# The opening of a decoder-block kernel: who casts the second weight tile, and in which order the first rows are turned

## The chip, the cores and the metric

The kernel runs on one core of one Trainium2 chip. The metric is device time in microseconds (us) of one execution; the time of a kernel is the median of several runs. Engines are named as the profile names them: PE is TensorE (matmuls; PEld its weight loads), DVE is VectorE, ACT is ScalarE, POOL is GpSimd, SP issues most of the DMAs.

## The reference, cut to what matters

One decoder block for 512 rows of 1024 numbers (float32): a convolution mixer and a linear recurrence side by side, merged by gates, then a SwiGLU layer. Only its beginning matters here:

```python
def rmsnorm(x, g):
    xf = x.astype(jnp.float32)
    y = xf * lax.rsqrt(jnp.mean(xf * xf, axis=-1, keepdims=True) + EPS)
    return (y * g.astype(jnp.float32)).astype(x.dtype)
...
    h = rmsnorm(x, norm1_g[l])
    z = h @ w_in[l] + b_in[l]
    z_glu, z_rx, z_rg, z_ga, z_gb = jnp.split(z, split_idx, axis=-1)
    u = z_glu[..., :D_CONV] * jax.nn.sigmoid(z_glu[..., D_CONV:])
    ...
```

## The kernel before, in words

Rows of `x` lie on partitions, four row tiles of 128 rows, each in two halves of 512 columns (`xt[t][h]`). The products need the normalised rows turned, so that the 1024 features lie on partitions: eight feature tiles `c` of 128, each a pair `h1p[c]` of a high part (float32 rounded to the PE's fp32r) and a low part (what the rounding left). Weights are split in the same way: a weight tile of 1024 x 128 is loaded into a `raw` buffer, cast to its high part, and the low part is the difference. A product of one feature tile is three matmuls: weight high by input high, weight high by input low, weight low by input high (24 matmuls for a weight tile).

The kernel's beginning is written out by hand inside `tc.manual_schedule(...)` (L640): in it the order of PE, ACT, DVE and SP is that of the Python code. POOL is left to the planner. After it, the planner orders the rest. The steps are:

1. `WARM = 21` matmuls of ones on ones (L505, 42 passes in the profile), which compute nothing that is used and stand ahead of all else on PE.
2. `norm1_rows(0)`, `norm1_rows(1)` (L591): ACT squares and sums each half (L550, L556), takes the root (L557), DVE inverts it (L558) and scales both halves of the row tile (L595, twice).
3. `rows_turned` (L513): the gain `norm1_g` is turned on PE (L517) and copied by DVE into `par` (L518).
4. `emit_to(1, vec.tensor_copy)`: the first weight tile's high part, cast by DVE (L123); its low part by POOL (L119).
5. `turn_half(..., 0, ...)` (L567) for row tiles 0 and 1: for each `c`, two transposes (L574), one for each row tile, then ACT writes the high part with the gain (L582) and DVE the low part (L583). Four PSUM banks take turns.
6. `emit_to(2, vec.tensor_copy, later)`: the second weight tile's high part, again cast by DVE; its low part is DVE's too, put between the two squares of row tile 2 (L652).
7. The loads of row tiles 2 and 3 and of the parameter rows (SP), `norm1_rows(2)`, `norm1_rows(3)`.
8. `early_mm(0, 0)`: 24 matmuls of the first weight tile on the first 256 rows, with the weight-low ones last; `early_mm(1, 0)`: the same for the second weight tile.
9. `turn_half(..., 1, ...)` for row tiles 2 and 3 (three PSUM buffers in turn), then `early_mm(0, 1)`, the recurrence's small factors, `early_mm(1, 1)`, and the rest of the parameters (L517).

Then the third weight tile follows, with all 512 rows in one matmul.

Of the kernel before, what the change touches and what calls it, by code (L numbers as in the profile page):

```python
# [26 lines left out]
ND = D // P  # L27
# [6 lines left out]
RAW = 4  # L34
HL = 5
AHEAD = 4
WARM = 21

FEW, MANY = 32, 112

# [46 lines left out]
def tile_block(ctx, tc, a, out):  # L87
# [19 lines left out]
    def bank(name):  # L107
        return psum.tile([P, T], F32, tag="mm", name=name)
# [4 lines left out]
    vec, act, pe, pool_e = nc.vector, nc.scalar, nc.tensor, nc.gpsimd  # L113
# [388 lines left out]


    wp = bank2("warm")
    for _ in range(WARM):  # L505
        pe.matmul(wp[:, :P], ones, ones, start=True, stop=True)  # L506

    first = [i for i, (lo, _, _) in enumerate(parts) if lo < n_first]
    load_x(0)
# [11 lines left out]
    def pc(name, i):  # L521
        return par[:, col[name] + i : col[name] + i + 1]


    def mm3(ps, ws, xs, lo_last=False):


        n = 3 * len(ws)
        i = 0
        three = [((wh, xh), (wh, xl), (wl, xh)) for (wh, wl), (xh, xl) in zip(ws, xs)]  # L530
        if lo_last:
            three = [q[:2] for q in three] + [q[2:] for q in three]
        for l, r in (q for qs in three for q in qs):
            pe.matmul(ps, l, r, start=i == 0, stop=i == n - 1)  # L534
            i += 1

    def w_tiles(key, kt, ahead=AHEAD):
        h, l = weights(key, ahead)
        return [(h[:, k, :], l[:, k, :]) for k in range(kt)]
# [21 lines left out]
    def rstd_of(halves, junk, between=None):  # L561
        begun = rstd_begin(halves[0], junk[0])
        if between:
            between()
        return rstd_end(begun, halves[1], junk[1])

    def turn_half(name, rows, gname, dest, hf, bk, some=range(ND), full=None):  # L567

        cs = slice(hf * 256, hf * 256 + 256)
        for c in some:  # L570
            ps = bk[c % len(bk)](f"{name}{hf}{c}")
            for t in range(2):
                src = rows[2 * hf + t][c // 4][:, (c % 4) * P : (c % 4 + 1) * P]
                pe.transpose(ps[:, t * P : (t + 1) * P], src, ident)  # L574
# [7 lines left out]
            act.activation(h, ps[:, :256], AF.Copy, scale=g)  # L582
            last = vec.scalar_tensor_tensor(out=l, in0=ps[:, :256], scalar=g, in1=h.bitcast(F32), op0=ALU.mult, op1=ALU.subtract)  # L583
# [7 lines left out]
    def norm1_rows(t, between=None):  # L591
        junk = [shortt(f"n1j{t}{h}") for h in range(2)]
        r = rstd_of(xt[t], junk, between)
        for h in range(2):
            vec.tensor_scalar(out=xt[t][h], in0=xt[t][h], scalar1=r, scalar2=None, op0=ALU.mult)  # L595

    HALVES = [slice(0, 256), slice(256, 512)]
    EARLY = 1
    EARLY_IN = [(GLU + j + 8 * o) for j in range(EARLY) for o in range(2)]
    early = []  # L600

    def early_mm(i, hf):
        m = EARLY_IN[i]
        if hf == 0:
            early.append((m, w_tiles(f"in{m}", ND, 0), bank(f"z{m}")))
        _, ws, ps = early[i]
        mm3(ps[:, HALVES[hf]], ws, parts_of(h1p, HALVES[hf]), lo_last=hf == 0)


    c4, c8 = (consts.tile([P, NR], F32, name=n) for n in ("c4", "c8"))  # L610
# [3 lines left out]
    def lru_factors(scratch):  # L614

        lam = par[:, col["lru_lambda"] : col["lru_lambda"] + NR]
        e, q, po, cc = (scratch[:, i * NR : (i + 1) * NR] for i in range(4))
        ab, s, s2 = (lru_t[:, i, :] for i in range(3))
        vec.tensor_scalar(out=e, in0=lam, scalar1=-1.0, scalar2=None, op0=ALU.mult)
        vec.tensor_tensor(out=ab, in0=lam, in1=e, op=ALU.max)  # L620
        act.activation(ab, ab, AF.Exp, scale=-1.0)
        for g, name in enumerate(("lru_ba", "lru_bx")):
            vec.tensor_scalar(out=bh[:, g, :], in0=par[:, col[name] : col[name] + NR], scalar1=0.5, scalar2=None, op0=ALU.mult)
        vec.tensor_scalar(out=q, in0=ab, scalar1=2.0, scalar2=None, op0=ALU.add)
        vec.reciprocal(q, q)
# [12 lines left out]

    ET = mybir.EngineType
    with tc.manual_schedule(engines={ET.PE, ET.Activation, ET.DVE, ET.SP}):  # L640
        norm1_rows(0)
        norm1_rows(1)
        rows_turned(0, ROWS[0][1])
        emit_to(1, vec.tensor_copy)
        turn_half("tx", xt, "norm1_g", h1p, 0, [bank, bank, bank, bank2])
        later = Later()
        emit_to(2, vec.tensor_copy, later)
        load_x(2)
        load_x(3)
        for i in first[1:]:  # L650
            load_rows(i)
        norm1_rows(2, lambda: vec.tensor_tensor(**later.operands))  # L652
        norm1_rows(3)
        for i in range(len(parts)):
            if i not in first:
                load_rows(i)
        early_mm(0, 0)
        early_mm(1, 0)
        turn_half("tx", xt, "norm1_g", h1p, 1, [bank2, bank, bank])
        emit_to(3)  # L660
        early_mm(0, 1)
        lru_factors(rows_turned(ROWS[0][1], n_first)[:, 2 * P :])
        emit_to(4)
        early_mm(1, 1)
        rows_turned(n_first, n_rows)
    h1 = parts_of(h1p)

# [623 lines left out]
```

## Time and profile before

| | |
|---|---|
| median of 3 runs | 797.87 us (797.6 to 798.1) |
| the profiled execution | 797.7 us |
| its span, first to last instruction | 795.9 us |
| PE busy | 789.2 us, 99% |
| DVE, ACT, POOL busy | 673.2, 471.7, 228.8 us |

The span is shorter than the time by what lies before the first and after the last instruction. PE's busy time counts a matmul until its modelled end, so that two in a row overlap; where PE starts its next matmul is the better clock. A row of the timeline gives the start in us from the span's start, the time until the group's last end, the engine and line, what is written from what, and in brackets how long the engine sat idle before it and what ended that.

### The profile page before, as it was taken

The numbers are of one execution on the slowest core, as the hardware profiler recorded it, in microseconds if no ns is written. First come the engines' busy times: TensorE is split into PE (matmuls) and PEld (weight loads), VectorE is DVE, ScalarE is ACT, GpSimd is POOL, SyncE is SP. The second block draws the span as 40 slices with busy tenths as digits, with TensorE's granted clock in tenths as the row PEclk, the third lists the DMA queues.
The fourth block names the chain that finished last, engine by engine and source line by source line (L and its number), as shares of the span: only waits on it lengthen the run. The fifth ranks groups of instructions, "written<-read, shape, count | busy, mean of one in ns | idle before, by whom it ended". The sixth has DMA issues, their size and how long they took to land.

```text
span 795.9 us, 12177 instructions
## 1 busy us (share of the span) xinstructions
PE 789.2 (99%) x4369; PEld 690.5 (87%) x4369; DVE 673.2 (85%) x1020; ACT 471.7 (59%) x683; POOL 228.8 (29%) x181
## 2 busy tenths in 40 slices
PE   9999999999999999999999999999999999999997
PEld 8888888888888888888888898999999999888885
DVE  6699899999989988786787889978878887889757
ACT  6646585987768855563335575545455555577443
POOL 1855766797666856030000000000000000000000
PEclk9999999999999999999999999999999999999999
DMA  6945646487555664368847545566555553676652
GB/s 213 257 130 143 187 144 208 121 247 208 173 168 173 213 182 120 128 203 263 276 160 243 172 134 158 131 171 181 155 133 133 133 133 106 210 258 207 198 173 106
DMA packets 184604, 140.29 MB, mean 176 GB/s; under 512 B 14259, under 2 KB 162143, under 8 KB 184543
## 3 DMA queue, kind: packets, MB, share of 16 engines
q1 hardware_dynamic: 183103, 134.27, 55.2%
q0 software_dynamic: 1440, 5.24, 3.5%
q8 instruction: 34, 0.56, 0.3%
q14 instruction: 27, 0.22, 0.1%
HBM read 113.79 MB, written 18.64 MB: 166 GB/s over the span
## 4 chain that ended last, share of the span: by engine, by line
PE 99%; DVE 0%; issue 0%; ACT 0%
PE z L534 36%; PE or L953 13%; PE ft L1080 7%; PE yb L534 7%; PE fa L1080 7%; PE fr L1080 6%; PE ya L534 5%; PE mxr L953 5%; PE fe L1080 4%; PE g L827 3%; PE fb L1080 2%; PE f L534 2%; PE warm L506 1%; PE f L1106 1%; PE tx L574 1%; PE th L574 0%
## 5 line engine op out<-in xcount | busy, mean ns | idle before, releaser
L702 DVE SCALAR_TENSOR_TENSOR cv<-u,par,cv 128x511 f32<-128x511 f32 (+19 forms) x240 | 162.4, 730 | 5.0 <-ACT cv L699 4.7
L119 POOL TENSOR_TENSOR hl_in<-raw_in,hl_in 128x1024 fp32r<-128x1024 f32 x51 | 123.5, 2426 | 83.1 <-ACT hl_in L123 69.6
L355 POOL DMA_DIRECT2D raw_fb<-raw_fb x10 | 8.7, 874 | 298.4 <-DVE raw_fb L357 186.1
L119 POOL TENSOR_TENSOR ows<-ows 128x256 f32<-128x256 f32 x66 | 56.7, 861 | 37.7 <-DMA ows<-in_ffn_w_dram 34.7
L123 ACT CAST hl_ft<-raw_fb 128x1024 fp32r<-128x1024 f32 x40 | 41.8, 1048 | 32.5 <-DVE raw_fb L357 17.0
L123 ACT CAST hl_in<-raw_in 128x1024 fp32r<-128x1024 f32 x50 | 52.1, 1043 | 10.4 <-PE z L534 6.6
L119 DVE TENSOR_TENSOR hl_ft<-raw_fb,hl_ft 128x1024 fp32r<-128x1024 f32 x40 | 48.5, 1220 | 7.0 <-ACT hl_ft L123 6.9
L119 DVE TENSOR_TENSOR hl_fb<-raw_fb,hl_fb 128x1024 fp32r<-128x1024 f32 x30 | 36.6, 1221 | 9.5 <-ACT hl_fb L123 9.3
L357 DVE TENSOR_TENSOR raw_fb<-raw_fb,raw_fb 128x1024 f32<-128x1024 f32 x20 | 24.5, 1225 | 20.3 <-DMA raw_fb<-in_ffn_w_dram 20.0
L534 PE MATMUL z<-h10h,hl_in 128*128 128x512 f32 (+1 forms) x108 | 41.5, 385 | 0.0
L534 PE MATMUL z<-h17h,hl_in 128*128 128x512 f32 (+1 forms) x108 | 41.1, 381 | 0.0
L534 PE MATMUL z<-h13h,hl_in 128*128 128x512 f32 (+1 forms) x108 | 41.1, 381 | 0.0
L534 PE MATMUL z<-h15h,hl_in 128*128 128x512 f32 (+1 forms) x108 | 41.1, 381 | 0.0
L534 PE MATMUL z<-h14h,hl_in 128*128 128x512 f32 (+1 forms) x108 | 41.1, 381 | 0.0
L534 PE MATMUL z<-h16h,hl_in 128*128 128x512 f32 (+1 forms) x108 | 41.1, 381 | 0.0
L534 PE MATMUL z<-h12h,hl_in 128*128 128x512 f32 (+1 forms) x108 | 41.1, 381 | 0.0
L534 PE MATMUL z<-h11h,hl_in 128*128 128x512 f32 (+1 forms) x108 | 41.1, 381 | 0.0
L123 ACT CAST hl_fb<-raw_fb 128x1024 fp32r<-128x1024 f32 x30 | 31.4, 1047 | 8.9 <-PE mxr L953 3.7
L119 DVE TENSOR_TENSOR hl_ob<-raw_ob,hl_ob 128x1024 fp32r<-128x1024 f32 (+1 forms) x23 | 27.0, 1174 | 11.0 <-ACT hl_ob L123 10.9
L123 ACT CAST hl_ob<-raw_ob 128x1024 fp32r<-128x1024 f32 (+1 forms) x23 | 23.3, 1015 | 21.6 <-PE or L953 10.8
L1080 PE MATMUL fe<-hs_0h,hl_ft 128*128 128x256 f32 x160 | 30.7, 283 | 0.0
L1080 PE MATMUL ft<-hs_1h,hl_ft 128*128 128x256 f32 x160 | 30.4, 283 | 0.0
(1016 smaller groups left out, 2610.0 us busy)
## 6 DMA issues: line engine op xcount, KB each, us to landing
raw_in<-in_w_in_dram SPq DMA_DIRECT2D x52, 512.0 KB
raw_fb<-in_ffn_w_dram SPq DMA_DIRECT2D x96, 256.0 KB
ows<-in_ffn_w_dram SPq DMA_DIRECT2D x44, 256.0 KB
os<-ows SPq DMA_DIRECT2D x22, 512.0 KB
raw_ob<-in_ffn_w_dram SPq DMA_DIRECT2D x33, 256.0 KB
raw_ot<-os SPq DMA_DIRECT2D x33, 256.0 KB
raw_lo<-in_lru_w_out_dram SPq DMA_DIRECT2D x16, 320.0 KB
raw_fb<-raw_fb POOLq DMA_DIRECT2D x10, 512.0 KB, 4.6
```

What stands on the lines that cost most here:

```text
L119: return eng.tensor_tensor(out=o, in0=x, in1=y, op=ALU.subtract)
L123: copy(h, full)
L355: pool_e.dma_start(out=q, in_=y, accum_op=ALU.add)
L357: vec.tensor_tensor(out=q, in0=q, in1=y, op=ALU.add)
L506: pe.matmul(wp[:, :P], ones, ones, start=True, stop=True)
L534: pe.matmul(ps, l, r, start=i == 0, stop=i == n - 1)
L574: pe.transpose(ps[:, t * P : (t + 1) * P], src, ident)
L702: vec.scalar_tensor_tensor(out=acc[c][:, s:], in0=u[c][:, : T - s], scalar=dw(c, s), in1=acc[c][:, s:], op0=ALU.mult, op1=ALU.add)
L827: pe.matmul(ps, l, r, start=k == 0, stop=k == len(mms) - 1)
L953: pe.matmul(banks[i], l_[:, ts], r_, start=start and n == 0, stop=stop and n == 2, skip_group_check=again)
L1080: pe.matmul(ps[:, HALVES[i]], lw[:, 4 * i + c, :], rx_, start=not (again or i or c or m), stop=bool(i and c == 3 and m == 2), skip_group_c ...
L1106: pe.matmul(plain_1[:, cs], l, r, start=k == 0 and m == 0, stop=k == ND - 1 and m == 2)
```

## The change

The warming matmuls are cut from 21 to 12 plus 3. After the first 12, the eight transposes of row tile 0 are issued as soon as its rows are scaled; then come the 3 other warming matmuls, the gain's transpose, and the eight transposes of row tile 1. Four PSUM banks hold all of it: bank `c % 4` has feature tile `c` and `c + 4`, each with both row tiles. Only then do ACT and DVE split them (`split_rows`), in the order of `c`.

The high part of the second weight tile is cast by POOL instead of DVE. POOL joins the engines whose order is written out: first this cast, then the low part of the first weight tile. DVE keeps the second tile's low part.

Matmuls of both weight tiles on the first 256 rows are mixed: four feature tiles of the first, then for each further feature tile of the first two of the second; the weight-low matmuls come after these, the second tile's first.

Row tiles 2 and 3 go through ACT and DVE in a slightly different order (`norm1_pair`: the sum of squares of row tile 3 is begun ahead of the scaling of row tile 2). Their transposes are also done row tile by row tile, all sixteen ahead of ACT's and DVE's split.

```diff
-WARM = 21
+WARM = 12, 3
...
-    for _ in range(WARM):
-        pe.matmul(wp[:, :P], ones, ones, start=True, stop=True)
+    def warm_up(n):
+        for _ in range(n):
+            pe.matmul(wp[:, :P], ones, ones, start=True, stop=True)
...
+    def norm1_pair(t, t2, later):
+        jk, jk2 = row_junk(t), row_junk(t2)
+        begun = rstd_begin(xt[t][0], jk[0])
+        vec.tensor_tensor(**later.operands)
+        r = rstd_end(begun, xt[t][1], jk[1])
+        begun = rstd_begin(xt[t2][0], jk2[0])
+        scale_rows(t, r)
+        scale_rows(t2, rstd_end(begun, xt[t2][1], jk2[1]))
...
+    def turn_rows(pairs, t):
+        for c in (0, 4, 1, 5, 2, 6, 3, 7):
+            at_ = (c // 4) * 256 + (t % 2) * P
+            pe.transpose(pairs[c % 4][:, at_ : at_ + P], xt[t][c // 4][:, (c % 4) * P : (c % 4 + 1) * P], ident)
+
+    def split_rows(pairs, hf):
+        for c in range(ND):
+            ps = pairs[c % 4][:, HALVES[c // 4]]
+            g = pc("norm1_g", c)
+            h, l = (v[:, HALVES[hf]] for v in h1p[c])
+            act.activation(h, ps, AF.Copy, scale=g)
+            vec.scalar_tensor_tensor(out=l, in0=ps, scalar=g, in1=h.bitcast(F32), op0=ALU.mult, op1=ALU.subtract)
...
-    with tc.manual_schedule(engines={ET.PE, ET.Activation, ET.DVE, ET.SP}):
+    with tc.manual_schedule(engines={ET.PE, ET.Activation, ET.DVE, ET.SP, ET.Pool}):
+        first_ps = [bank(f"tx0{i}") for i in range(ND // 2)]
+        low0, low1 = Later(), Later()
+        warm_up(WARM[0])
         norm1_rows(0)
+        turn_rows(first_ps, 0)
+        warm_up(WARM[1])
         norm1_rows(1)
         rows_turned(0, ROWS[0][1])
-        emit_to(1, vec.tensor_copy)
-        turn_half("tx", xt, "norm1_g", h1p, 0, [bank, bank, bank, bank2])
-        later = Later()
-        emit_to(2, vec.tensor_copy, later)
+        turn_rows(first_ps, 1)
+        emit_to(1, vec.tensor_copy, low0)
+        split_rows(first_ps, 0)
+        emit_to(2, pool_e.tensor_copy, low1)
+        pool_e.tensor_tensor(**low0.operands)
         load_x(2)
         load_x(3)
...
-        norm1_rows(2, lambda: vec.tensor_tensor(**later.operands))
-        norm1_rows(3)
+        norm1_pair(2, 3, low1)
...
-        early_mm(0, 0)
+        order = [(0, k, m) for k in range(4) for m in range(2)]
+        for k in range(4, ND):
+            order += [(i, q, m) for i, q in ((0, k), (1, 2 * k - 8), (1, 2 * k - 7)) for m in range(2)]
+        early_mm(0, order + [(i, k, 2) for i in (1, 0) for k in range(ND)])
+        next_ps = [b(f"tx1{i}") for i, b in enumerate((bank2, bank2, bank, bank))]
+        turn_rows(next_ps, 2)
+        turn_rows(next_ps, 3)
+        split_rows(next_ps, 1)
+        emit_to(3)
         early_mm(1, 0)
-        turn_half("tx", xt, "norm1_g", h1p, 1, [bank2, bank, bank])
-        emit_to(3)
-        early_mm(0, 1)
         lru_factors(rows_turned(ROWS[0][1], n_first)[:, 2 * P :])
-        emit_to(4)
         early_mm(1, 1)
+        emit_to(4)
         rows_turned(n_first, n_rows)
```

In the changed code the first argument of `early_mm` is the half of the rows, and the second an order of matmuls or a weight tile.

More of the change, by code (lines that the diff above doesn't have):

```diff
@@ L589, in tile_block, with row_junk, scale_rows, norm1_rows @@
     h1p = [pairt(f"h1{c}") for c in range(ND)]
-    def norm1_rows(t, between=None):
-        junk = [shortt(f"n1j{t}{h}") for h in range(2)]
-        r = rstd_of(xt[t], junk, between)
+    def row_junk(t):
+        return [shortt(f"n1j{t}{h}") for h in range(2)]
+    def scale_rows(t, r):
         for h in range(2):
             vec.tensor_scalar(out=xt[t][h], in0=xt[t][h], scalar1=r, scalar2=None, op0=ALU.mult)
+    def norm1_rows(t):
+        scale_rows(t, rstd_of(xt[t], row_junk(t)))
+    def norm1_pair(t, t2, later):
[6 more added lines that the diff above has]
+        scale_rows(t2, rstd_end(begun, xt[t2][1], jk2[1]))
@@ L597, in tile_block @@
     HALVES = [slice(0, 256), slice(256, 512)]
-    EARLY = 1
-    EARLY_IN = [(GLU + j + 8 * o) for j in range(EARLY) for o in range(2)]
+    EARLY_IN = (GLU, GLU + 8)
     early = []
[L602 to L607, printed above, removed]
+    def turn_rows(pairs, t):
+        for c in (0, 4, 1, 5, 2, 6, 3, 7):
+            at_ = (c // 4) * 256 + (t % 2) * P
+            pe.transpose(pairs[c % 4][:, at_ : at_ + P], xt[t][c // 4][:, (c % 4) * P : (c % 4 + 1) * P], ident)
@@ new lines, in split_rows, with early_mm @@
+    def split_rows(pairs, hf):
[5 more added lines that the diff above has]
+            vec.scalar_tensor_tensor(out=l, in0=ps, scalar=g, in1=h.bitcast(F32), op0=ALU.mult, op1=ALU.subtract)
+    def early_mm(hf, order):
+        if not early:
+            early.extend((m, w_tiles(f"in{m}", ND, 0), bank(f"z{m}")) for m in EARLY_IN)
+        if order in (0, 1):
+            order = [(order, k, m) for k in range(ND) for m in range(3)]
+        left = [3 * ND] * len(early)
+        for i, k, part in order:
+            _, ws, ps = early[i]
+            (wh, wl), (xh, xl) = ws[k], (v[:, HALVES[hf]] for v in h1p[k])
+            l, r = ((wh, xh), (wh, xl), (wl, xh))[part]
+            left[i] -= 1
+            pe.matmul(ps[:, HALVES[hf]], l, r, start=left[i] == 3 * ND - 1, stop=not left[i])
@@ L656, in tile_block @@
                 load_rows(i)
-        early_mm(0, 0)
+        order = [(0, k, m) for k in range(4) for m in range(2)]
[7 more added lines that the diff above has]
+        emit_to(3)
         early_mm(1, 0)
-        turn_half("tx", xt, "norm1_g", h1p, 1, [bank2, bank, bank])
-        emit_to(3)
-        early_mm(0, 1)
         lru_factors(rows_turned(ROWS[0][1], n_first)[:, 2 * P :])
+        early_mm(1, 1)
         emit_to(4)
-        early_mm(1, 1)
         rows_turned(n_first, n_rows)
```

## The prediction

> **What bounds the kernel now.** I read the page's totals first, then the chain of work that ended last for its first 30 us, then the timeline of the same stretch.
>
> ```profile
> PE 789.2 (99%) x4369; PEld 690.5 (87%) x4369; DVE 673.2 (85%) x1020; ACT 471.7 (59%) x683; POOL 228.8 (29%) x181
> 1.09 7.80 PE warm L506 x42
> 8.89 0.15 PE par_ps L517
> 9.04 1.90 PE tx L574 x16
> 10.94 6.51 PE z L534 x48
> 17.45 2.13 PE tx L574 x16
> 19.58 2.87 PE z L534 x24
> 22.44 0.07 PE par_ps L517
> 22.52 2.92 PE z L534 x24
> 25.43 0.29 PE par_ps L517 x3
> 25.72 43.59 PE z L534 x192
> ```
>
> The last row is 192 matmuls at 43.59 / 192 = 0.227 us, back to back. All that this change can win or lose directly lies ahead of it, in the first 25.5 us. In there 24 products with nothing to wait for take 2.92 us (0.12 us each), but the 48 of the first half take 6.51 where 48 x 0.12 = 5.8 would do; the 42 warming passes fill the time until row tiles 0 and 1 are scaled; and sixteen transposes, 1.90 and 2.13 us, stand between. The details:
>
> ```profile
> 5.69 0.89 DVE L595 TENSOR_SCALAR x<-x,stats 128x512 f32<-128x512 f32 x2
> 5.81 0.63 ACT L550 ACTIVATE n1j<-x 128x512 f32<-128x512 f32 x1 [0.36 <-DMA x<-in_x_dram]
> 7.83 0.88 DVE L595 TENSOR_SCALAR x<-x,stats 128x512 f32<-128x512 f32 x2
> 9.08 0.17 DVE L518 COPY par<-par_ps 128x8 f32<-128x8 f32 x1 [0.37 <-PE par_ps L517]
> 9.16 0.68 DVE L123 CAST hl_in<-raw_in 128x1024 fp32r<-128x1024 f32 x1
> 9.45 0.47 ACT L582 ACTIVATE h10h<-tx,par 128x256 fp32r<-128x256 f32 x1 [1.85 <-PE tx L574]
> 9.96 0.48 DVE L583 SCALAR_TENSOR_TENSOR h10l<-tx,par,h10h 128x256 fp32r<-128x256 f32 x1
> 10.70 0.36 PE L534 MATMUL z<-h10h,hl_in 128*128 128x256 f32 x1
> 12.71 0.47 DVE L583 SCALAR_TENSOR_TENSOR h17l<-tx,par,h17h 128x256 fp32r<-128x256 f32 x1
> 13.10 0.68 DVE L123 CAST hl_in<-raw_in 128x1024 fp32r<-128x1024 f32 x1
> 13.82 1.23 DVE L652 TENSOR_TENSOR hl_in<-raw_in,hl_in 128x1024 fp32r<-128x1024 f32 x1
> 16.72 0.88 DVE L595 TENSOR_SCALAR x<-x,stats 128x512 f32<-128x512 f32 x2
> 17.28 2.30 PE L574 MATMUL tx<-ident,x 128*128 128x128 f32 x16
> 17.70 0.47 ACT L582 ACTIVATE h10h<-tx,par 128x256 fp32r<-128x256 f32 x1 [1.22 <-PE tx L574]
> 18.21 0.48 DVE L583 SCALAR_TENSOR_TENSOR h10l<-tx,par,h10h 128x256 fp32r<-128x256 f32 x1 [0.61 <-ACT h10h L582]
> 19.14 0.20 PEld L574 LDWEIGHTS tx<-ident,x 128*128 128x128 f32 x2 [0.19 <-DVE h11l L583]
> 19.33 0.36 PE L534 MATMUL z<-h10h,hl_in 128*128 128x256 f32 x1
> 20.96 0.47 DVE L583 SCALAR_TENSOR_TENSOR h17l<-tx,par,h17h 128x256 fp32r<-128x256 f32 x1
> 22.16 0.28 PE L534 MATMUL z<-h17h,hl_in 128*128 128x256 f32 x1
> ```
>
> DVE makes the eight low parts of a half at a pace of (12.71 - 9.96) / 7 = 0.39 us, against two products of 0.12 each: that is why the first weight tile's first sixteen products are paced. In the second half the transposes end late, since buffers come free only after DVE (19.14, waiting for h11l), and PE begins its products at 19.33.
>
> **The change, part by part.** I follow the new order with these durations.
>
> Warming. The trace shows the pace of the warming passes and its change (windows restricted to them: us, PE busy, count):
>
> ```profile
> 1.00:7.00 6.00, 5.91 (x27) 1.00 0.81 254
> 7.00:8.70 1.70, 1.70 (x17) 1.00 1.17 316
> L506 PEld LDWEIGHTS warm<-ones x42: 192/333/333, 1.1 to 8.5; 128*128 128x128 f32 x42
> ```
>
> Until about 7.0 a pass takes 5.91 / 27.5 = 0.215 us, after it about 0.11; a weight load 333 ns, then 192. So PE runs at about half speed for the first 5.9 us of work and then doubles, although the column of the granted clock says 1.00. Twelve matmuls are 24 passes: 1.09 + 24 x 0.215 = 6.25. Row tile 0's first half is scaled at 5.69 + 0.45 = 6.14 and its second at 6.58, so there is next to no gap: transposes at 6.3, 6.6, 6.8, and from 7.0 at 0.12 (1.90 / 16), the last at 7.5. The six passes of the other warming end near 8.3, the gain's transpose starts at 8.4.
>
> Row tile 1 is scaled at 8.27 and 8.71: only 8 transposes now follow it, from 8.55 to 9.6, where 16 ran until 10.9. DVE copies the gain right behind its scaling (8.73 instead of 9.08), so its cast of the first weight tile runs from 8.9 to 9.6, ACT starts at 8.95 (before 9.45), and the first low part starts at 9.65 (before 9.96). The first product starts at 9.65 instead of 10.70. DVE's pace puts the fifth low part at 9.65 + 4 x 0.39 + 0.48 = 11.7, so the tenth product, which needs it, starts there.
>
> From there the second tile's products fill the pauses, if its high part is ready by 11.85. The trace of before has no cast on POOL. Its data: 2.1 MB must land ahead (four halves of row tiles of 256 KB, two weights of 512 KB); at the rates of
>
> ```profile
> 0.00:4.50 4.50, 3.41 (x16) 1.00 0.53 166
> 0.00:9.00 9.00, 7.91 (x44) 1.00 0.80 239
> ```
>
> 0.75 MB are moved at 4.5 us, while row tile 1's first half (0.79 MB) is there at 5.81, a lag of 1.2 us; 2.15 MB are moved at 9.0, so the second tile is there near 10.2 to 10.5. The cast's price lies between these rows:
>
> ```profile
> L215 POOL MEMSET raw_gate<- x10: 524/527/533, 34.6 to 209.0; 128x512 f32 x10
> 9.93 2.40 POOL L119 TENSOR_TENSOR hl_in<-raw_in,hl_in 128x1024 fp32r<-128x1024 f32 x1 [8.62 <-DVE hl_in L123]
> ```
>
> A memset of half the size writes alone: 2 x 0.53 = 1.05 us. A difference reads two operands: 2.40. A cast reads one; I take 1.15, near the memset, as reading and writing can run side by side where two reads of one path cannot. Then the cast ends at 11.65 and costs PE nothing; at 2.40 it ends at 12.9 and holds PE for 1.05 us, since products are issued in order. [...] The first tile's low part moves behind the cast on POOL, 11.65 to 14.05 instead of 9.93 to 12.33; it is needed by the 41st product, at about 15.4. With DVE's two-input difference beside it, it could stretch by that 1.23 us and still be in time.
>
> From the tenth product on PE is dense: 11.7 + 39 x 0.12 = 16.4 for the end of the 48 (before 17.28). DVE without the cast (0.68) and begun 0.3 earlier makes the second tile's low part from 13.05 to 14.3, needed by the 33rd product at 14.5. Row tiles 2 and 3 are then scaled by about 15.75 and 16.9 (ACT's squares, one after the other from 12.0, set these). Tile 2 is ready when PE comes at 16.4, and tile 3 when its turn comes at 17.35.
>
> What this gains is partly given back: transposing row by row, ACT must see the ninth transpose instead of the second. Before, ACT began 0.42 us after the first transpose (17.28 to 17.70); now 16.4 + 7 x 0.12 + 0.42 = 17.66. So ACT's and DVE's chain is where it was, and DVE ends h17l near 21.4. But the sixteen transposes no longer wait for buffers; PE is through by 18.4 and follows DVE: after h17l two products are left, ending 21.4 + 0.04 + 2 x 0.12 = 21.7, where 22.28 stood before (22.16 + 0.12). The 24 products of the second tile and the parameters follow unchanged. The third weight tile and SP's queue:
>
> ```profile
> 21.74 2.39 POOL L119 TENSOR_TENSOR hl_in<-raw_in,hl_in 128x1024 fp32r<-128x1024 f32 x1 [9.41 <-ACT hl_in L123]
> 15.55 1.33 SPq L167 DMA_DIRECT2D raw_in<-in_w_in_dram  x2
> ```
>
> ACT's chain stays where it was, so the third tile's low part still ends at 24.1, needed at 25.3. SP keeps the order of its transfers at the beginning, so no load starts later; the third load counted from 15.55 reuses the first tile's buffer and waits for POOL's difference, but that is through at 14.05, before SP comes to it. **The sum: 22.28 - 21.7 = 0.6 us, against the execution's own 797.7: 797.1.** The median of the runs shown is 0.17 above this execution; I say 797.2. That is 0.07%, below the 0.2% that a measurement of this kernel tells from no change.
>
> The sum moves one to one with the end of the 48 products, T: the gain is about 17.0 - T. The earliest T is 9.65 + 5.8 = 15.4, but then row tile 3, ready in its first half at 16.4, holds the ninth transpose, and the gain is 1.0 at most. With the cast at 2.40, T is 17.45 and the loss 0.45.
>
> **Rivals.**
> (a) The clock. Before, PE doubled its pace after 5.9 us of unbroken matmuls. Now these stop after 5.2 us, and transposes follow. If transposes do not keep the release on its way, PE stays slow: eight transposes at 0.215 until 8.1, six passes until 9.4, the gain and eight transposes until 11.2, and the products begin 1.55 later than in my sum, each at 0.215 to 0.23 instead of 0.12. With a release another 5.9 us later, at 17.1, 26 products are through by then and the other 22 end at 19.8: a loss of 2.8, 800.5 us. With a release after 3 us of products, T is 18.4 and the loss 1.4. In between, 800.0. It decides for slower if the release comes later than about 14.5. For it: the doubling at 7.0 is on the page, and nothing shows what brings it about. Against: transposes keep PE as busy as matmuls do, and the second set (17.28, 2.30 us) leaves the pace at 0.12. [...] The trace agrees with a release after sustained work (7.0) and cannot test the transposes.
> (b) The change is made and the gain does not come: the cast at or near 2.40, or DVE's and POOL's reads in each other's way, T near 17: 797.7, up to 798.2. For it: no cast on POOL in the trace. Against: a memset's 0.53 for half.
> (c) The planner's later orders differ on DVE, ACT and SP for the first quarter of their work. PE was dense there (43.59 for 192), so it can only lose: one weight tile late by a few us. If so, 800. Against it stands this group, in which POOL idled before its differences for want of ACT's casts, not of data:
>
> ```profile
> L119 POOL TENSOR_TENSOR hl_in<-raw_in,hl_in 128x1024 fp32r<-128x1024 f32 x51 | 123.5, 2426 | 83.1 <-ACT hl_in L123 69.6
> ```
>
> (d) Faster by more than 0.2% would need 1.6 us, and I find 1.0 at most; it is left for what the trace does not price.
>
> **How the numbers follow.** My forecast, 797.2 with its own range of 796.6 to 797.7, has 0.48; (b) 0.16; both are within 0.2%, together 0.64. (a) has 0.22 and (c) 0.04, both slower: 0.26. (d) 0.10. The range starts below the greatest gain (797.7 - 1.0, less 0.3 for the spread of runs) at 796.3, and reaches into (a) to 799.8, which leaves its worse half, (c) and most of (d) out.
>
> **What would show it.** Right: warming until 6.3, a doubled pace near 7.0 still (weight loads of 333 then 192 ns or less), the first product near 9.65, POOL's cast near 1.15 us from about 10.5, the 48 products ended near 16.4 with no gap after the tenth, ACT's first split of the second half near 17.7, the third weight tile's first product at 24.9 instead of 25.52. Wrong: products spaced at 0.21 or more after 10 us (a); PE waiting for POOL's cast (b); a gap in the 192 matmuls that follow (c).

## The result, and the profile after

The changed kernel takes 799.48 us (median of 22 runs, 798.33 to 801.62), the kernel before 797.78 (22 runs, 797.22 to 798.78): 1.0021 times the time before by the medians, 1.002 with a 95% interval of 1.0013 to 1.0026 by the comparison. The change costs 1.7 us, where the prediction had a gain of 0.6. The profiled execution of the changed kernel took 799.46 us, with a span of 797.7.

Two rows of its page (totals; DMA queues: packets, megabytes, share):

```profile
PE 789.0 (99%) x4357; PEld 689.5 (86%) x4357; DVE 672.3 (84%) x1019; ACT 472.1 (59%) x683; POOL 228.9 (29%) x182
q8 instruction: 34, 0.56, 0.3%
```

PE was busy 789.2 us before and 789.0 now, with 12 passes fewer; the loss is idle time. The rows of PE line up one to one behind the opening, so the two traces can be laid over each other: the changed kernel is 0.56 us late at the third weight tile (26.08 for 25.52), 0.44 at the last product ahead of 541 us (541.05 for 540.61), 1.66 at the next one (542.39 for 540.73), and 1.77 at the last matmul. So there are two losses, one in the opening and one of 1.2 us at 541 us.

**The opening.** The timeline of the changed kernel (start, us, engine):

```profile
6.64 1.29 PE L621 MATMUL tx<-ident,x 128*128 128x128 f32 x8
7.77 0.83 PE L508 MATMUL warm<-ones 128*128 128x128 f32 x6
8.69 1.09 PE L621 MATMUL tx<-ident,x 128*128 128x128 f32 x8
9.93 0.36 PE L644 MATMUL z<-h10h,hl_in 128*128 128x256 f32 x1
10.86 1.04 POOL L123 CAST hl_in<-raw_in 128x1024 fp32r<-128x1024 f32 x1 [9.55 <-DMA raw_in<-in_w_in_dram]
11.87 2.40 POOL L690 TENSOR_TENSOR hl_in<-raw_in,hl_in 128x1024 fp32r<-128x1024 f32 x1
12.91 2.44 DVE L607 TENSOR_TENSOR hl_in<-raw_in,hl_in 128x1024 fp32r<-128x1024 f32 x1
15.41 0.38 PE L644 MATMUL z<-h10h,hl_in 128*128 128x256 f32 x1 [0.56 <-DVE hl_in L607]
17.43 1.80 PE L621 MATMUL tx<-ident,x 128*128 128x128 f32 x15
18.72 0.47 ACT L629 ACTIVATE h10h<-tx,par 128x256 fp32r<-128x256 f32 x1 [2.85 <-PE tx L621]
```

The cast on POOL takes 1.04 us. POOL's difference takes 2.40, as before. But DVE's difference, which took 1.23 before, takes 2.44: it starts at 12.91, POOL's ends at 14.27, and DVE's ends 1.08 later, at 15.35. PE has by then issued all that needs no low weights, and waits 0.56 for the 33rd product. So the transposes of the second half start at 17.43 (17.28 before). The chain of the same stretch goes on from there:

```profile
15.41 2.18 PE z L644 x16
17.59 1.10 PE tx L621 x10
...
18.72 0.48 ACT h10h L629
...
19.77 3.25 PE z L644 x23
23.02 0.07 PE par_ps L519
23.09 2.91 PE z L644 x24
```

ACT begins when ten transposes are through, 1.29 us after the first, and the 24 products end at 23.02 (22.44 before).

**The pause at 541 us.** The waits of PE behind the opening, from 25 us on (what waited for what: us in total, times, longest us); the kernel before has no row at all in this view:

```profile
PE fr L1127 <- ACT ft L1227: 1.1, 1, 1.1
```

This lies in the SwiGLU layer, where the two programs do the same. Followed back, each link comes later: ACT's cast, DVE's sum of two buffers (L357: 523.78 instead of 522.15), SP's loads into the buffers it adds (519.72 instead of 518.23), which wait for a buffer that one of POOL's accumulating transfers (L355, 512 KB added from one buffer into another) holds. The DMA view of 514 to 519 us, first of the kernel before, then of the changed one (busy tenths of the engines in 40 slices; queues; issues, with the time to landing):

```profile
DMA  0000000099591991959909969199010000000000
q0 software_dynamic: 144, 0.52, 55.4%
raw_fb<-raw_fb POOLq DMA_DIRECT2D x1, 512.0 KB, 4.6
```

```profile
DMA  0000000000793990959909839199093020100101
q0 software_dynamic: 143, 0.52, 55.3%
q8 instruction: 1, 0.02, 1.8%
raw_fb<-raw_fb POOLq DMA_DIRECT2D x1, 512.0 KB, 5.7
```

The transfer lands 5.7 us after its issue instead of 4.6. It begins 0.3 us later, most of it is through after as long as before, and then a few packets trail with nearly all engines idle (the 3020100101 at the end). In its time falls one packet of 16 KB on the instruction queue. There are 34 of these in a run, one for every 2 x 4357 / 34 = 256 records of PE (a matmul pass and its weight load are a record each). I take them for PE's own program, fetched as it goes. Since the change takes 2 x 12 records out ahead of it, the fetches come 24 records later in the program, and the one that stood at 513.76 stands at 515.33. Whether that delays the transfer is what the experiments ask.

### The profile page after: what moved, and what is told of

Read it like the earlier page. It is cut to its first block, busy times and chain, and to the rows that moved or that the text cites. A ratio compares the mean times of both kernels' runs of the same rounds, so it can differ in the third digit from the quotient of the medians.

```text
span 797.7 us, 12154 instructions
## 1 busy us (share of the span) xinstructions
PE 789.0 (99%) x4357; PEld 689.5 (86%) x4357; DVE 672.3 (84%) x1019; ACT 472.1 (59%) x683; POOL 228.9 (29%) x182
## 4 chain that ended last, share of the span: by engine, by line
PE 91%; DMA 4%; DVE 3%; ACT 1%; issue 0%; SPq 0%; DVEq 0%; POOLq 0%; ACTq 0%
PE z L536 34%; PE or L1000 13%; PE yb L536 7%; PE fa L1127 6%; PE ft L1127 6%; PE ya L536 5%; PE mxr L1000 5%; PE g L874 3%; PE fr L1127 3%; PE fe L1127 3%; PE fb L1127 2%; PE f L536 1%; DMA raw_fb<-raw_fb 1%; DMA raw_fb<-in_ffn_w_dram 1%; PE z L644 1%; DMA raw_in<-in_w_in_dram 1%
## 5 line engine op out<-in xcount | busy, mean ns | idle before, releaser
L749 DVE SCALAR_TENSOR_TENSOR cv<-u,par,cv 128x511 f32<-128x511 f32 (+17 forms) x240 | 162.2, 729 | 5.3 <-ACT cv L746 5.1
L119 POOL TENSOR_TENSOR hl_in<-raw_in,hl_in 128x1024 fp32r<-128x1024 f32 x50 | 120.7, 2417 | 73.8 <-ACT hl_in L123 67.5
L355 POOL DMA_DIRECT2D raw_fb<-raw_fb x10 | 8.7, 875 | 299.5 <-DVE raw_fb L357 187.6
L357 DVE TENSOR_TENSOR raw_fb<-raw_fb,raw_fb 128x1024 f32<-128x1024 f32 x20 | 24.5, 1225 | 20.8 <-DMA raw_fb<-in_ffn_w_dram 20.5
L536 PE MATMUL z<-h10h,hl_in 128*128 128x512 f32 x100 | 39.1, 391 | 0.0
L536 PE MATMUL z<-h11h,hl_in 128*128 128x512 f32 x100 | 38.9, 389 | 0.0
L536 PE MATMUL z<-h13h,hl_in 128*128 128x512 f32 x100 | 38.9, 389 | 0.0
L536 PE MATMUL z<-h12h,hl_in 128*128 128x512 f32 x100 | 38.9, 389 | 0.0
L536 PE MATMUL z<-h14h,hl_in 128*128 128x512 f32 x100 | 38.9, 389 | 0.0
L536 PE MATMUL z<-h15h,hl_in 128*128 128x512 f32 x100 | 38.9, 389 | 0.0
L536 PE MATMUL z<-h16h,hl_in 128*128 128x512 f32 x100 | 38.9, 389 | 0.0
L536 PE MATMUL z<-h17h,hl_in 128*128 128x512 f32 x100 | 38.9, 389 | 0.0
```

Source lines behind the costliest of these rows:

```text
L119: return eng.tensor_tensor(out=o, in0=x, in1=y, op=ALU.subtract)
L355: pool_e.dma_start(out=q, in_=y, accum_op=ALU.add)
L357: vec.tensor_tensor(out=q, in0=q, in1=y, op=ALU.add)
L749: vec.scalar_tensor_tensor(out=acc[c][:, s:], in0=u[c][:, : T - s], scalar=dw(c, s), in1=acc[c][:, s:], op0=ALU.mult, op1=ALU.add)
```

## The experiments

Three questions: is the pause at 541 a matter of where the fetch falls, what makes the opening late, and do the two add up to the loss.

**again**, the changed kernel once more.

> The changed kernel once more, for a second trace. The first one lost 0.57 us in its opening and 1.2 us at 541 us, where a transfer issued by POOL had taken 5.7 us in place of 4.6. If that transfer is long by chance, this trace has its own pattern: the opening again 0.5 to 0.7 us later than before's, the place at 541 with or without a gap, and a time of 798.3 plus the gaps that it shows. If the new opening brings the long transfer about, the gap of 1.2 us stands at 541 again. In both cases DVE's difference for the second weight tile takes 2.4 us.

799.33 us, ratio 1.002 (1.0011 to 1.0028). The pause is there again with the same 1.1 us; the opening is 0.24 late. So the opening of one kernel differs by 0.3 us between two executions, and a difference of one trace from another in it is no surer than that.

**before_later**, the kernel before with more warming.

```diff
-WARM = 21
+WARM = 24
```

> The kernel before with 24 warming matmuls in place of 21: six passes of 0.11 us more, so that everything after them starts about 0.65 us later, as after the change, with none of the change in it. If the lateness alone brings the gap at 541 about: 1.5 to 2.0 us slower than before, with that gap in the trace. If the gap comes from the changed orders of the planner, or by chance in equal parts in both: 0.4 to 0.7 us slower.

797.80 us, ratio 1.0002 (0.9993 to 1.0011), and no pause. It was not later, though: PE's pace doubled earlier in its profiled execution (48 passes took 7.28 us, where 42 had taken 7.80), and its third weight tile came 0.50 early.

**before_less_code**, the kernel before with less warming, so that its program is as short as the changed one's.

```diff
-WARM = 21
+WARM = 15
```

> The kernel before with 15 warming matmuls in place of 21: twelve passes fewer, so 24 PE records fewer (12 weight loads, 12 matmuls), as in the changed kernel, and nothing else of the change. Four traces of the changed kernel and its variants fetch 16 KB of PE's code about 24 records later in the program than before's, at about 515 and 531 us, in the middle of the transfers that POOL issues at 514 and 529. If these fetches cause the gap at 541 (theory): it stands in this trace too, with a fetch near 515, and the kernel is 0.8 to 1.6 us slower than before. If the changed orders of DVE, ACT and SP cause it, or chance: no gap, and the time is before's within 0.3 us (the opening waits for row tile 1 as it did). If PE is still slow at 9 us because it idled after the warming: 0.5 to 2 us are lost ahead of 26 us, which is a loss of its own.

799.28 us, ratio 1.0019 (1.0009 to 1.0028). Waits of PE from 25 us on:

```profile
PE fr L1080 <- ACT ft L1180: 1.7, 2, 1.5
```

The pause appears in the kernel before, with nothing of the change in it but 24 records less, and with a second one of 0.15. This kernel loses in its opening too (0.73 in its trace): PE runs out of warming at 6.85 and stands still, and then its transposes run at half pace (15 in 3.40 us, where 16 took 1.90):

```profile
8.92 3.40 PE L574 MATMUL tx<-ident,x 128*128 128x128 f32 x15 [1.00 <-DVE x L595]
```

**same_code**, the changed kernel with 24 records put back by splitting six of the first twelve warming matmuls in two of 64 columns each.

```diff
-        warm_up(WARM[0])
+        half_warm(12)
+        warm_up(WARM[0] - 6)
```

> The changed kernel with as many PE records as before: six of its first twelve warming matmuls are each made into two that move 64 columns, which adds 24 records and no columns. If the place of the code fetches causes the gap at 541 (theory): the transfers that POOL issues at 514 and 529 are not both long, the gap is gone or under 0.4 us, and the time is 0.6 to 1.4 us below the changed kernel's, at 798.0 to 798.6; what is left is the opening. If the planner's orders cause it: the gap of 0.9 to 1.2 us stays, and the time is the changed kernel's.

800.09 us, ratio 1.0024 (1.0014 to 1.0033). The pause is gone, but the opening is 2.57 late. This padding has a cost of its own:

```profile
1.08 5.38 PE L512 MATMUL warm<-ones 128*128 128x64 f32 x24 [1.08 <-DVE ones L499]
6.26 2.88 PE L508 MATMUL warm<-ones 128*128 128x128 f32 x12
8.93 1.89 PE L625 MATMUL tx<-ident,x 128*128 128x128 f32 x8
```

A pass of half the columns takes as long as a whole one (5.38 / 24 = 0.224 us), so warming lasted 2.6 us longer; and the doubling of the pace, at some 7 us before, came near 10.7.

**before_again**, the kernel before, profiled once more.

> The kernel before once more, for a second trace of it. If the fetch of PE's code near 513.8 us lies ahead of the data of the transfer that POOL issues at 513.6 by the order of the program, it does so again (before the data begins at 515), that transfer lands after 4.2 us, and there is no gap at 541. If its place there was chance: another place, and perhaps a gap.

This one execution took 799.13. Waits of PE from 25 us on:

```profile
PE g L827 <- DMA ext6h<-xb7h: 0.7, 1, 0.7
PE fr L1080 <- ACT ft L1180: 0.6, 1, 0.6
```

So the kernel before has the pause too, now and then, and another one at 180 us for a transfer.

**pad_wait**, the changed kernel with 24 records put back where PE waits anyway, ahead of the 33rd product; "pad" in the order stands for `tiny(6)`.

```diff
+    def tiny(n):
+        for _ in range(n):
+            pe.matmul(wp[:8, :8], ones[:, :8], ones[:, :8], start=True, stop=True)
...
-        early_mm(0, order + [(i, k, 2) for i in (1, 0) for k in range(ND)])
+        early_mm(0, order + ["pad"] + [(i, k, 2) for i in (1, 0) for k in range(ND)])
```

> The changed kernel with six matmuls of 8 columns by 8 put where TensorE waits for the second weight tile's low part (before the 33rd product): 24 TensorE records, as many as the change takes out of the program ahead of 500 us; warming is left alone. Theory (the pause at 541 us comes with the place of TensorE's instruction fetch, which 24 records fewer move by some 1.4 us into a transfer): the opening is as the changed kernel's or up to 0.3 us later, the fetches near 514 and 529 us stand as before the change, the pause at 541 is mostly gone, 798.2 to 798.8. Rival (something else that the change does later, such as VectorE's and SyncE's orders, makes the pause): pause as in the changed kernel, 799.5 to 799.9.

798.12 us, ratio 1.0004 (0.9996 to 1.0013). Six matmuls that compute nothing save 1.3 us, by the two ratios. Its timeline, and its DMA view of 514 to 519 us:

```profile
15.12 0.45 PE L512 MATMUL warm<-ones 128*8 128x8 f32 x12
```

```profile
DMA  0040000000079199091990935919909301000000
q8 instruction: 1, 0.02, 1.1%
raw_fb<-raw_fb POOLq DMA_DIRECT2D x1, 512.0 KB, 4.6
```

The opening is as late as the changed kernel's (0.65). The fetch is the single 4 at the left, ahead of the transfer's data, the transfer lands after 4.6 us, and PE has no wait behind the opening.

What the traces say of the second of the ten transfers of L355, the fetch nearest to it, and the pause (times from the packets of the traces, in us; transfers from issue to the end of their last packet; "fetch" is its end against the start of the transfer's data, negative when it was through before):

| kernel | PE records against before | fetch | 2nd, 3rd transfer | pause at 541 |
|---|---|---|---|---|
| before | 0 | -0.37 | 4.19, 5.30 | none |
| before_again | 0 | -0.03 | 5.11, 5.49 | 0.6 |
| before_later | +12 | +0.04 | 5.37, 4.20 | none |
| after | -24 | +1.39 | 5.36, 5.76 | 1.1 |
| again | -24 | +1.59 | 5.68, 5.87 | 1.1 |
| lows_on_dve | -24 | +1.26 | 5.19, 5.09 | 0.4 |
| turn_pairs | -24 | +0.68 | 4.72, 5.76 | 0.9 |
| quad_order | -24 | +1.31 | 5.40, 5.63 | 1.0 |
| before_less_code | -24 | +1.75 | 5.84, 6.17 | 1.5 |
| same_code | 0 | -0.26 | 4.21, 5.46 | none |
| three_mended | 0 | -0.10 | 4.84, 5.61 | 0.8 |
| pad_wait | 0 | -0.33 | 4.22, 4.81 | none |
| lows_pad | 0 | -0.53 | 4.20, 5.02 | none |
| lows_order_pad | 0 | -0.48 | 4.20, 4.62 | none |
| banks | -24 | +0.78 | 4.77, 6.11 | 1.2 |
| lows_banks | -24 | +1.38 | 5.47, 5.28 | 0.6 |
| lows_banks_pad | 0 | -0.22 | 4.36, 4.90 | none |

(The kernels not met so far are told below.) A transfer whose fetch is through 0.2 us ahead of its data takes 4.2 us. Over the second to fourth transfers of all 17 traces, 7 are of this kind (4.19 to 4.36), and the other 44 all took 4.60 or more. Over all ten transfers of each trace, the 111 that no fetch meets (none in the 0.2 us ahead of the data or beside it) took 4.19 to 4.36, the 59 that meet one 4.27 to 6.17. Where both the second and the third are late, PE pauses: in all eight traces with 24 records less, in two of the nine with the old number or more. The engine that I take to fetch does not wait for it (PE has no wait behind the opening in the kernel before's trace, with 34 such packets); the transfer beside it lands later (5.36 us in the changed kernel's trace, 4.19 in the kernel before's). Why packets of the transfer then trail is not shown, and no view here shows which engine carried the fetch.

**lows_on_dve**, the changed kernel with both low parts on DVE; POOL only casts.

```diff
-        pool_e.tensor_tensor(**low0.operands)
...
-        vec.tensor_tensor(**later.operands)
+        for low in later:
+            vec.tensor_tensor(**low.operands)
```

> The changed kernel, but the first weight tile's low part is made by DVE right behind the second's, and POOL only casts, so that no difference of POOL's stands beside DVE's. If the two engines' reads hold each other up (theory): DVE's difference takes 1.23 us again, the 33rd matmul no longer waits 0.56 us, the 48 end near 16.6 in place of 17.4, and the opening ends 0.5 to 0.9 us earlier than the changed kernel's, near or a little ahead of before's. If DVE's difference was long for another reason (the data of the transfer landing beside it): it stays at 2.4 us, and the first tile's low part, now behind it, costs about 1 us more.

798.99 us, ratio 1.0012 (1.0003 to 1.0021). Rows of its timeline:

```profile
13.06 2.36 DVE L608 TENSOR_TENSOR hl_in<-raw_in,hl_in 128x1024 fp32r<-128x1024 f32 x2
16.70 1.91 PE L622 MATMUL tx<-ident,x 128*128 128x128 f32 x16
17.99 0.47 ACT L630 ACTIVATE h10h<-tx,par 128x256 fp32r<-128x256 f32 x1 [2.06 <-PE tx L622]
```

Two differences on DVE take 2.36, less than one took beside POOL's. PE no longer waits, the transposes start 0.73 earlier than in the changed kernel, and the third weight tile comes 0.17 ahead of the kernel before's trace instead of 0.56 behind. The transfers beside the two differences are those of the changed kernel (0.03 MB from 12.9 to 15.4 us in both traces), so that they were not what made one long; same_code says the same, where POOL's difference was through (14.91) before DVE's began (15.79) and DVE's took 1.23.

**turn_pairs**, the changed kernel with the second half's transposes issued feature tile by feature tile, as before the change.

```diff
-        turn_rows(next_ps, 2)
-        turn_rows(next_ps, 3)
+        for c in range(ND):
+            for t in (2, 3):
+                at_ = (c // 4) * 256 + (t % 2) * P
+                pe.transpose(next_ps[c % 4][:, at_ : at_ + P], ...)
```

> The changed kernel, with the second half's sixteen transposes in pairs again (feature tile by feature tile, both row tiles), still all ahead of the split and in four banks. If waiting for the ninth transpose costs what the prediction said (0.84 us): ACT starts the second half's split about 0.5 us behind the first transpose in place of 1.3, and the opening ends about 0.8 us earlier than the changed kernel's (near 25.2, before's 25.5). If something else sets ACT's start, for one row tile 3 scaled too late: less than 0.3 us.

799.17 us, ratio 1.0013 (1.0004 to 1.0021). Its chain:

```profile
17.67 1.11 PE tx L707 x10
...
18.80 0.48 ACT h10h L629
```

Nothing gained: ACT still waits for ten transposes, although the two that it reads come first. The tenth is the last one into that bank, which holds feature tiles 0 and 4.

**banks** and **lows_banks**: the changed kernel, and lows_on_dve, with feature tiles 2k and 2k + 1 in a bank in the second half, so that four transposes complete one.

```diff
+        for c in range(0, ND, 2):
+            for t in (0, 1):
+                for d in (c, c + 1):
+                    at_ = (d % 2) * 256 + t * P
+                    pe.transpose(pairs[c // 2][:, at_ : at_ + P], ...)
```

> The changed kernel with column tiles 2k and 2k+1 in one PSUM bank in the second half (instead of c and c+4), and each bank's four transposes issued together. Theory (ScalarE waits for the last transpose into the bank that it reads, the 10th in the changed kernel): it now waits for the fourth, so its first split starts 0.6 us earlier (0.66 after the first transpose instead of 1.29), the third weight tile's first product 0.5 earlier, near 25.5; the pause at 541 stays; 798.9. Rival (ScalarE waits for something else): its first split stays 1.3 us behind the first transpose and the time at 799.5.

> The same, and both low parts made by VectorE one after the other, so that GpSimd only casts. Theory (the changed kernel's opening loses to two things, VectorE standing still behind GpSimd's difference and ScalarE's wait for the 10th transpose): with both mended the third weight tile's first product comes near 24.9, where the prediction had it, 0.6 us ahead of the kernel before; the pause at 541 stays: 798.4. If the two don't add up: 25.3 to 25.5 and 798.9.

804.97 us, ratio 1.009 (1.0077 to 1.0104), and 804.86, 1.0086 (1.0073 to 1.01). ACT did start earlier (18.37 and 17.65), and then this, in the timeline of banks:

```profile
18.37 0.47 ACT L638 ACTIVATE h10h<-tx,par 128x256 fp32r<-128x256 f32 x1 [2.20 <-PE tx L623]
19.39 0.48 ACT L638 ACTIVATE h11h<-tx,par 128x256 fp32r<-128x256 f32 x1 [0.55 <-DVE h10l L639]
19.77 0.47 ACT L638 ACTIVATE h12h<-tx,par 128x256 fp32r<-128x256 f32 x1
20.82 0.47 ACT L638 ACTIVATE h13h<-tx,par 128x256 fp32r<-128x256 f32 x1 [0.58 <-DVE h12l L639]
```

ACT does not read a bank here while DVE reads its other half (it waits for DVE's h10l, h12l): the two take turns, 1.43 us for two feature tiles instead of 0.72. The third weight tile of banks came 2.76 late, late transfers made PE wait at 185 us (another 2.9), and the pause at 541 is there as well (1.2). I had not seen that the old layout, with c and c + 4 together, keeps two neighbours in different banks. The waits of turn_pairs (ACT for the tenth transpose, ten in 1.11 us) and of banks (0.55 to 0.58 us for DVE at the other half) go by bank here and not by tile.

**quad_order**, the changed kernel with its banks, and the transposes issued bank by bank.

```diff
-        turn_rows(next_ps, 2)
-        turn_rows(next_ps, 3)
+        for c in (0, 4, 1, 5, 2, 6, 3, 7):
+            for t in (2, 3):
+                ...
```

> The changed kernel with the banks left as they are (column tiles c and c+4 together) and the second half's transposes issued bank by bank (0, 4, 1, 5, 2, 6, 3, 7, each for row tiles 2 and 3). If ScalarE waits for the last transpose into its bank, it starts 0.65 to 0.75 us behind the first transpose instead of 1.29, and the third weight tile's first product comes 0.3 to 0.5 earlier, near 25.7; the pause at 541 stays: 799.0 to 799.2. If the wait is for something else: 1.29 and 799.5.

798.97 us, ratio 1.0016 (1.0007 to 1.0024). From its timeline and its chain:

```profile
18.13 0.47 ACT L629 ACTIVATE h10h<-tx,par 128x256 fp32r<-128x256 f32 x1 [2.20 <-PE tx L707]
```

```profile
17.66 1.75 PE tx L707 x16
19.41 3.16 PE z L644 x24
22.56 0.07 PE par_ps L519
```

ACT starts 0.63 behind the first transpose (17.50), not 1.29. It is off the chain now; PE's products follow the transposes at once and end 0.46 earlier than in the changed kernel's trace (22.56 for 23.02). The pause stays (1.0).

**Together.** Four kernels mend more than one thing. **three_mended** is lows_on_dve with the padding of same_code and the order of quad_order; **lows_banks_pad** is lows_banks with six small matmuls among the first paced products; **lows_pad** is lows_on_dve with `tiny(6)` behind the first product; **lows_order_pad** is that with the order of quad_order.

> The changed kernel with three things mended together: both low parts on DVE, as many PE records as before, and the second half's transposes in the order 0 4 1 5 2 6 3 7 with both row tiles for each, so that the first bank is full after four transposes. That ACT waits for the tenth transpose whatever their order, as the pairs in the order 0 1 2 ... showed, means that it waits for the whole bank. If that reading is right: ACT starts 0.4 us behind the first transpose, but not before row tile 3 is scaled (17.4), so at 17.7 to 17.8, and the opening ends at 24.8 to 25.2 in place of before's 25.5; with no gap at 541 the time is 0.2 to 0.8 us below before's. If the bank is not the cause, ACT starts 1.1 us behind the first transpose again and the time is before's within 0.3 us.

> The same, and 24 TensorE records put back as six small matmuls in the pauses of the first paced products. Theory (all three losses mended): third weight tile near 25.0, no pause at 541 in most executions: 797.2 to 797.6, at or a little below the kernel before. If the place of the instruction fetch is not what makes the pause: 798.4 to 798.7.

> The changed kernel with both low parts on VectorE and six matmuls of 8 columns by 8 in VectorE's wait behind the first product, for the 24 TensorE records; nothing else. If the losses add up: third weight tile near 25.4, no pause at 541 in most executions: 797.6 to 797.9, no difference from the kernel before. If the pause comes back or the opening does not hold: 798.6 to 799.0.

> The same with the second half's transposes bank by bank: third weight tile 0.3 earlier, near 25.1, no pause at 541: 797.3 to 797.6, at most 0.06% below the kernel before.

three_mended took 800.07 us, ratio 1.0027 (1.0018 to 1.0037): it has the padding of same_code (opening 1.62 late), and its fetch was through only 0.1 us ahead of the data, so that the pause is there (0.8). lows_banks_pad took 804.85, 1.0091 (1.0079 to 1.0104), with the loss of banks; its small matmuls, put singly between the paced products, cost 0.17 us in each place (their pace went from 0.39 to 0.56). lows_pad took 797.52 us, ratio 0.9996 (0.9987 to 1.0005), and lows_order_pad 797.68, 0.9998 (0.9989 to 1.0008). The chain of lows_pad:

```profile
9.97 0.29 PE z L651
10.27 0.38 PE warm L512 x12
10.65 6.26 PE z L651 x47
16.91 1.11 PE tx L626 x10
...
18.04 0.48 ACT h10h L634
```

With DVE's difference clear of POOL's and the 24 records back, the whole loss of 1.7 us is gone. That is as far as it goes: no version beats the kernel before by more than the measurement can tell. The order of quad_order shows no gain on top of it: lows_order_pad's trace has a third weight tile 0.06 behind the kernel before's and a wait of 0.3 at 181 us. Its first product came at 10.36, lows_pad's at 9.88, so that this one trace does not tell what the order is worth there.

## Why the prediction was wrong

**The cast on POOL, the first product.** Right: 1.04 us from 10.86 (1.15 from 10.5 predicted), and nothing waited for it. 1.15 was a choice between 1.05 and 2.40 for which the kernel before had no row; its reason fits what came: one operand read and one written take 1.04, as writing alone does (2 x 0.53), and two read take 2.40. The first product came at 9.93 instead of 9.65.

**T, the end of the 48 products.** Here the sum failed: 17.43, not 16.4. The step that failed is that DVE "makes the second tile's low part from 13.05 to 14.3, needed by the 33rd product at 14.5". I had asked what DVE's difference does to POOL's, and given POOL 1.23 us of slack; it is DVE that stands still until POOL is through. In the six traces in which the two overlap (after, again, turn_pairs, quad_order, pad_wait, banks) DVE's ended 1.08 to 1.09 us after POOL's, whenever it had begun; without POOL's, T was 16.70. The other 0.3 of the miss is the late first product. The traces show the wait (2.44 us for 1.23), not what the two engines have in common that brings it about.

That DVE is the one to wait is no rule. In each of the six traces POOL's had begun first. In three_mended DVE's cast began 0.03 us ahead of POOL's, and there it is POOL's that is long, 1.56 instead of 1.04:

```profile
10.84 0.68 DVE L123 CAST hl_in<-raw_in 128x1024 fp32r<-128x1024 f32 x1
10.87 1.56 POOL L123 CAST hl_in<-raw_in 128x1024 fp32r<-128x1024 f32 x1 [9.56 <-DMA raw_in<-in_w_in_dram]
```

Here, then, the engine that began second waited, in either direction; no run reverses the order of the two differences. The step could have been read ahead of the result, since the trace of the kernel before has such a pair at 297 us: a DVE instruction that took 0.69 us just ahead of it (at 296.29) takes 2.77 beside POOL's difference and ends 0.5 us after it.

```profile
296.73 2.51 POOL L119 TENSOR_TENSOR hl_in<-raw_in,hl_in 128x1024 fp32r<-128x1024 f32 x1 [1.02 <-ACT hl_in L123]
297.01 2.77 DVE L725 TENSOR_TENSOR lnmt<-lnmt,u 128x512 f32<-128x512 f32 x1
```

**ACT's start.** Its distance from the first transpose was right (1.26 predicted, 1.29 measured), in part by luck, since the prediction has ACT wait for the ninth transpose and it waits for the tenth. quad_order's chain shows that it was on the path; the 0.46 between the two traces is what it may have cost, little more than the 0.3 by which two executions of the changed kernel differ. It was taken for a matter of the row-by-row order; turn_pairs shows that it is one of the banks.

**The end of the opening.** 21.7 was predicted for the end of the 24 products, counted as the last one's start and 0.12, and 24.9 for the third weight tile; 22.85 (22.73 and 0.12) and 26.08 came. Of these 1.2 us 1.03 is T; the rest is mostly that PE's products set the end and not DVE's last low part, which was there at 22.45 while its product began at 22.57. So of the 2.3 us between forecast and measurement about half is the opening and half the pause.

**Rival (a), the clock.** Not seen in any trace of the changed kernel: the first eight transposes take 7.77 - 6.64 = 1.13 us, a doubling on the way, and the products are spaced at 0.12. The doubling came during or before the transposes, at the end of 5.49 us of warming passes or behind them, so whether transposes put it off is not tested here. It does move from execution to execution: 24 warming passes took 5.49 us in the changed kernel and 4.66 in lows_pad, and 42 took 7.80 and 7.07 in two executions of the kernel before, whose openings differ by 0.5.

**Rival (b)** named "DVE's and POOL's reads in each other's way, T near 17", and priced it at 797.7 to 798.2. For the opening alone this is what happened: pad_wait, where the rest is taken away, measures 798.12.

**Rival (c)** said 800 for a late tile further on. The size is right by luck; mechanism and place are not. Nothing was late by the planner's orders: in pad_wait DVE, ACT, POOL and SP have the changed kernel's orders to the last instruction, and PE has no wait behind the opening. That the loss is 1.7 and not 0.4 comes from the fetch of PE's program, which no step of the prediction had: twelve passes were counted as time in the opening, not as bytes of a program whose fetches stand beside transfers 500 us later.

**The range.** 799.48 lies inside 796.3 to 799.8 by luck: the upper part was there for the clock, which was not seen. (Its lower end, the greatest gain and 0.3 below 797.7, is 796.4 when added up.)

What stays open: why a fetch costs the transfer 0.4 to 2.0 us where its own packet takes 0.9 to 1.9, and why the one in before_again and before_later, over just as the data began, still cost 0.9 and 1.2. That a fetch in the transfer's time delays it is shown by records taken out (before_less_code) and put back (pad_wait); the way in which it does is not shown.

## What to carry to other kernels

When work moves from one engine to another, look for every pair of instructions of DVE and POOL that now overlap, and ask which of the two begins second: here that one waited (DVE's difference took 2.44 us instead of 1.23, POOL's cast 1.56 instead of 1.04); the trace at hand may already have such a pair. Ask of a PSUM bank who writes it last and who else reads it, not only of the tile: the order of the transposes alone moved ACT's start from 1.29 to 0.63 us behind the first one (quad_order), and the layout took the split from 0.72 to 1.43 us for two feature tiles (banks). And in a kernel that is dense to 99%, a difference of 0.2% can come from the length of the program itself (24 records put back saved 1.3 us in pad_wait): before such a result is put down to the edit, take out or put back instructions that do nothing.

## What the runs showed of the hardware that I had not expected

- VectorE's difference of 128x1024 float32 makes next to no headway while a GpSimd difference begun before it runs: 2.44 us instead of 1.23, ending 1.08 after GpSimd's. A GpSimd cast begun 0.03 us behind a VectorE cast took 1.56 instead of 1.04. VectorE's splits, which read one operand from PSUM, keep their pace of 0.39 beside the same GpSimd instruction (11.87 to 12.91).
- The packets that I take for TensorE's program are of 16 KB, one per 256 records, each 0.9 to 1.9 us long beside these transfers, and a 512 KB transfer that meets one lands 0.1 to 2.0 us late (59 of 170; the others took 4.19 to 4.36).
- Warming passes of 64 columns take as long as those of 128 (0.224 us), and TensorE's pace doubled late behind them, near 10.7 us in same_code and near 9.0 in three_mended; that the narrow passes are the cause is not shown. Twelve passes of 8 columns take 0.38 together.
- In this program ScalarE and VectorE take turns at the two halves of one PSUM bank, each waiting for the other's instruction: 1.43 us for two feature tiles instead of 0.72.
